# A fourth expert with 64 token slots, large and small experts in strict alternation, and a general path per expert

## The chip, the cores and the metric

The kernel runs on one core of a Trainium2 chip. The metric is device time in microseconds (us) of one execution. Three executions of the kernel before took 1542.57, 1547.81 and 1548.6 us (median 1547.81). The execution whose trace is read here took 1543.95 us; its span, from the first to the last instruction, is 1542.2 us, so 1.75 us lie around the span.

## The reference

Two decoder layers over 256 positions of width 1024, in float32. Layer 0 has dilated attention and a dense mixer, layer 1 has windowed attention with sinks and a mixer of eight experts, of which each token takes two:

```python
def _moe(h, w_router, w1, w3, w2):
    logits = (h @ w_router).astype(jnp.float32)
    top_v, top_i = lax.top_k(logits, TOP_K)           # 2 of 8
    wts = jax.nn.softmax(top_v, axis=-1)
    gates = jnp.einsum('bske,bsk->bse', one_hot(top_i, N_EXPERTS), wts)
    y = jnp.zeros_like(h)
    for e in range(N_EXPERTS):
        y = y + gates[..., e:e + 1] * _swiglu(h, w1[e], w3[e], w2[e])   # (silu(h w1) * (h w3)) w2
    return y
```

Each expert has w1 and w3 of 1024 x 3584 and w2 of 3584 x 1024, 42 MiB in all. The 256 tokens make 512 choices, 64 per expert on average. On the inputs of the reference the experts 0 to 7 get 65, 75, 60, 89, 63, 65, 47 and 48 tokens. After the experts comes a gated projection of a per-layer embedding and a last RMSNorm.

## The kernel before, in words

Both layers run on one core, stage after stage. The change touches the last stage, the experts, which begins about 617 us into the span and ends about 1492 us.

**Slots and ranks.** `route` counts the tokens of each expert and ranks the experts by that count; expert 0 always stands at rank 0, and the others follow from the fullest down. `CAPS` gives each rank its slots, 96 or 64: five ranks have 96 and three 64. `TURNS` is the order in which ranks take their turn: 0, 5, 1, 2, 6, 3, 4, 7. With L for 96 slots and S for 64 that is L S L L S L L S.

**A turn.** `Expert.gather` picks an expert's tokens with one-hot matmuls (tile P, result xb). `hidden` multiplies them by w1 and w3 (result H), `hidden_tail` applies silu and the product and transposes (tiles sa, sb, hT), `output` multiplies by w2 (result Y), `combine` scatters Y back to the tokens (tiles yh, yl, PT) and adds it to x. The 3584 columns are done in four chunks, three of 1024 and one of 512; `hidden` of a chunk runs ahead of `output` of the chunk before. The tokens are the stationary operand, in groups of 32: a matmul of `mm32` holds 32 tokens and streams a weight tile's columns past them, and four of them run side by side on the array. A turn with 96 slots has three groups and three banks of H, one with 64 has two groups and two banks.

**Weights.** Each weight goes over the array straight from its load buffer (`next_raw`). A tile is 1 MiB, 42 per turn. The buffers are `raw` (5), `mwa` (2) and `mwb` (10). SyncE (SP in the trace) issues all loads in one order, each into the buffer that comes free next. In the last turn the pool `mwb` ends (`moe_cut`), so that the last 14 tiles of the experts and the four of the gate projection go through 7 buffers. Which expert a rank is, SyncE reads from the tensor `cnt` (`find`).

**The general path.** If any expert has more tokens than its slots (`most > 0`), `beyond(1)` goes over all eight experts again for the tokens left over, and `beyond(2)` once more if over 96 are left. Every engine loads `most` and branches. An engine that skips the branch waits on its own semaphores and adds to them what the branch would have added; SyncE waits there for all of its loads issued so far.

**Order.** `Flow` lays out the instructions by planned times while the program is built: TensorE's order (H, Y, gathers, combines) is fixed then, and each wait is a semaphore. SyncE's loads have no planned time; they follow as buffers come free.

Of the kernel before, what the change touches and what calls it, by code (L numbers as in the profile page):

```python
# [13 lines left out]
I32 = mybir.dt.int32  # L14
AF = mybir.ActivationFunctionType
OP = mybir.AluOpType
# [4 lines left out]
S = 256  # L21
# [7 lines left out]
MOE_CHUNKS = ((0, 1024), (1024, 1024), (2048, 1024), (3072, 512))  # L29
NE = 8  # L30

CAPS = (96, 96, 96, 96, 96, 64, 64, 64)
TURNS = (0, 5, 1, 2, 6, 3, 4, 7)
CAP = 96
BIG = 512.0
NRAW = 5
# [308 lines left out]
def trunk(ctx, tc, x, p, attn_norm, ffn_norm, a_w_qkv, a_w_o, kv_norm, kv_w, b_w_q, b_sinks,  # L345
          b_w_o, dense_w1, dense_w3, dense_w2, moe_router, moe_w1, moe_w3, moe_w2,
          ple_norm, ple_w_gate, ple_w_proj, final_norm, masks, rope, mats, lessm, out):
    nc = tc.nc
    ctx.enter_context(tc.manual_schedule())
    flow = Flow()  # L350
    scal = Timed(flow, "act", nc.scalar, act_cost)
    act = scal.activation
    vec = Timed(flow, "vec", nc.vector, vec_cost)
# [10 lines left out]
    def pool(name, bufs, stack=ctx, **kw):  # L364
        return stack.enter_context(tc.tile_pool(name=name, bufs=bufs, reuse_waits="tile", **kw))
# [7 lines left out]
    rt = pool("rt", 1)  # L373
# [4 lines left out]
    st = Stream(nc, scal, vec, flow, rawp, 3, 2048)  # L378
# [39 lines left out]
    def add_moe(s, seq, at=None, extra=None):  # L418


        prev = None
        where = 0

        for j, item in enumerate(list(seq) + [None]):
            if item is not None:
                e, f0, fn = item
                r0 = f0 * D // fn
                for r in range(0, D, s.width * 128 // fn):
                    for w in (moe_w1, moe_w3):
                        s.add((expert_tile(w, e, (r0 + r) * fn // 128, s.width), s.width // fn), "raw")  # L430
            if j == at:
                s.add(extra, "raw")
                where = len(s.specs)
            if prev is not None:
                e, f0, fn = prev
                for r in range(f0, f0 + fn, s.width * 128 // D):
                    s.add((expert_tile(moe_w2, e, r * D // 128, s.width), s.width // D), "raw")
            prev = item
        return where

    def moe_seq(es):
        return [(e, f0, fn) for e in es for f0, fn in MOE_CHUNKS]
# [486 lines left out]
    if True:  # L929
# [122 lines left out]
        posm = rt.tile([128, NB, NE], F32, name="posm")  # L1052
        gates = rt.tile([128, NB, NE], F32, name="gates")
        rstat = rt.tile([128, 8], F32, name="rstat")
        cnt = rt.tile([128, 16], I32, name="cnt")
        by_rank = [rt.tile([128, NB, NE], F32, name=n) for n in ("posr", "gater")]
        count, total, capx, capt = (rt.tile([128, NE], F32, name=n) for n in ("count", "total", "capx", "capt"))
        for r, c in enumerate(CAPS):
            vec.memset(capt[:, r:r + 1], float(c))
# [254 lines left out]
    def experts(es, nxt=None, then={}, ahead=True):  # L1314

        E = {}
        nf = len(MOE_CHUNKS)

        def begin(i):
            E[i] = es[i]()  # L1320
            return E[i].gather()

        def products(i, res, f, Y):
            if i == len(es) - 1 and f == nf - 1:

                flow.until(lambda: res)
                st.hold = False
            output(E[i], Y, res, MOE_CHUNKS[f][1], f == 0, f == nf - 1)
            if f == nf - 1:
                flow.start(E[i].combine(Y, nxt if i == len(es) - 1 else None))  # L1330

        prev = None
        for i in range(len(es)):
            if i not in E:
                g = begin(i)
                if not E[i].ready:
                    flow.spawn(g)
            Y = [psY.tile([128, 512], F32, name=f"Y{k}", tag=f"Y{k}") for k in (range(3) if E[i].ng == 3 else (0,))]
            for f, (f0, fn) in enumerate(MOE_CHUNKS):
                res = []  # L1340
                g = begin(i + 1) if ahead and f == nf - 2 and i + 1 < len(es) else None
                hidden(E[i], fn, res)
                if (i, f) in then:
                    then[i, f]()
                if not ahead:
                    products(i, res, f, Y)
                    continue
                if g is not None:
                    flow.spawn(g)
                if prev is not None:  # L1350
                    products(*prev)
                prev = (i, res, f, Y)
            if not ahead:
                flow.drain()
        if ahead:
            products(*prev)
        flow.drain()

    def route():

        while 0 not in n_f1.chosen:
            yield flow.now + 100.0
        yield flow.due(sel)
        ps = acc()
        mm(ps[:, 0:8], tri, sel[:, 0], start=True, stop=False, skip_group_check=True)
        mm(ps[:, 8:16], ones, sel[:, 0], start=False, stop=False, skip_group_check=True)
        mm(ps[:, 16:24], ones, sel[:, 0], start=False, stop=False, skip_group_check=True)
        while 1 not in n_f1.chosen:
            yield flow.now + 100.0
        yield flow.due(sel)  # L1370
        mm(ps[:, 8:16], tri, sel[:, 1], start=False, stop=False, skip_group_check=True)
        mm(ps[:, 16:24], ones, sel[:, 1], start=False, stop=True, skip_group_check=True)
        vec.scalar_tensor_tensor(posm.rearrange(g16), sel.rearrange(g16), -BIG, ps[:, 0:16], op0=OP.mult, op1=OP.add)
        if WARM2:
            warm(WARM2)
        first.append(Expert(CAPS[0], posm[:, :, 0:1], by_rank[1][:, :, 0:1]))
        vec.tensor_copy(count, ps[:, 16:24])
        flow.start(first[0].gather())

        d8, a8, perm = d4[:, 0], a4[:, 0], d4[:, 1]  # L1380
        vec.tensor_copy(total, count)
        vec.memset(total[:, 0:1], 2.0 * S)
        vec.tensor_tensor(d8, total[:, None, :].to_broadcast([128, NE, NE]),
                          total[:, :, None].to_broadcast([128, NE, NE]), op=OP.subtract)
        d, a = d8.rearrange(f64), a8.rearrange(f64)
        vec.scalar_tensor_tensor(a, d, 0.0, less, op0=OP.is_equal, op1=OP.mult)
        vec.scalar_tensor_tensor(a, d, 0.0, a, op0=OP.is_gt, op1=OP.add)
        vec.tensor_reduce(rstat[:, 0:8], a8, axis=AX.X, op=OP.add)
        vec.tensor_scalar(rstat[:, 0:8], rstat[:, 0:8], -BIG, None, op0=OP.add)

        vec.tensor_tensor(perm, iota[:, 0:8][:, :, None].to_broadcast([128, NE, NE]),
                          rstat[:, None, 0:8].to_broadcast([128, NE, NE]), op=OP.is_equal)
        vec.tensor_tensor(a8, perm, iota[:, None, 0:8].to_broadcast([128, NE, NE]), op=OP.mult)
        vec.tensor_reduce(rstat[:, 0:8], a8, axis=AX.X, op=OP.add)
        vec.tensor_scalar(cnt[:, 0:8], rstat[:, 0:8], BIG, None, op0=OP.add)
        for tb in range(NB):
            vec.tensor_tensor(a8, perm, posm[:, tb, None, :].to_broadcast([128, NE, NE]), op=OP.mult)
            vec.tensor_reduce(by_rank[0][:, tb], a8, axis=AX.X, op=OP.add)

        vec.tensor_tensor(a8, perm.rearrange("p r e -> p e r"), capt[:, None, :].to_broadcast([128, NE, NE]), op=OP.mult)  # L1400
        vec.tensor_reduce(capx, a8, axis=AX.X, op=OP.add)
        vec.tensor_tensor(total, count, capx, op=OP.subtract)
        vec.tensor_reduce(rstat[:, 0:1], total, axis=AX.X, op=OP.max)
        vec.tensor_scalar(cnt[:, 8:9], rstat[:, 0:1], 0.0, None, op0=OP.max)

    def find_gates():

# [31 lines left out]
    def find():  # L1439

        for r in TURNS:
            if r:
# [8 lines left out]
    banks.close()  # L1451


    most = nc.values_load(cnt[0:1, 8:9], min_val=0, max_val=S,
                          skip_runtime_bounds_check_because="a count of at most 256 tokens")
    main = st

    def beyond(i):

        nonlocal st, selp  # L1460
        sel1 = selp
        with ExitStack() as es:
            selp = pool(f"sel_{i}", 1, es, side="right")
            expert_pools(es, es, f"_{i}")
            st = Stream(nc, scal, vec, flow, pool(f"raw_{i}", 2, es, side="right"), 0, 1024, 2)
            for item in moe_seq(range(NE)):
                add_moe(st, [item])
            for tb in range(NB):
                vec.tensor_tensor(posm[:, tb], posm[:, tb], capx, op=OP.subtract)
            if i == 1:  # L1470
                vec.memset(capx, float(CAP))
            experts([lambda e=e: Expert(CAP, *(v[:, :, e:e + 1] for v in (posm, gates))) for e in range(NE)], ahead=False)
        st = main
        selp = sel1

# [154 lines left out]
```

## Time and profile before

| | |
|---|---|
| three executions, us | 1542.57, 1547.81, 1548.6 |
| profiled execution, us | 1543.95 |
| its span, us | 1542.2 |
| mean granted TensorE clock | 0.99 |
| TensorE (PE) busy | 1500.6 us, 97% |
| VectorE (DVE) busy | 541.3 us, 35% |
| ScalarE (ACT) busy | 435.2 us, 28% |
| moved by DMA | 455.66 MB, mean 295 GB/s |

PE is the matmul itself and PEld the loading of its stationary operand. Matmul ends are modelled, so the pace of a group is read from its starts. Each matmul of `mm32` in the program stands twice in the trace. "SPq" is SyncE's queue of DMA issues. A wait is put down to the event that came last.

### The profile page before, as it was taken

To read this page: it belongs to the slowest core of one execution; us is meant where nothing else is said; L and a number is where in the kernel's file an instruction comes from. 1 tells how busy PE (TensorE), PEld (TensorE's weight loads), DVE (VectorE), ACT (ScalarE), POOL (GpSimd) and SP (SyncE) were. 2 spreads that over 40 slices of the span, in tenths; PEclk is the share of its full clock that TensorE was granted. 3 is DMA by queue.
4 is the path that set the end of the run, shared out by engine and by line. 5 is a ranking of instruction groups with operands and counts; after the bars stand their busy time and mean duration, and the time that the engine had idled before them with its cause. 6 is when DMAs were issued, how large, how long until landed. Compare 5 with 4: busy or idle time off the path is not lost.

```text
span 1542.2 us, 28405 instructions
## 1 busy us (share of the span) xinstructions
PE 1500.6 (97%) x11944; PEld 859.4 (56%) x11944; DVE 541.3 (35%) x1274; ACT 435.2 (28%) x852; POOL 11.3 (1%) x22
## 2 busy tenths in 40 slices
PE   7999999999999999799999999999999999999977
PEld 7999988888888887334324333334343343343335
DVE  6777777755454796210020100210201001201124
ACT  5555555564443766110000100110100010001124
POOL 0000000000000000000000000000000000000000
PEclk9999999999999999899999999999999999999988
DMA  9554444475455331999999999999999999999780
GB/s 280 157 144 139 129 123 148 134 276 186 170 186 197 134 113 55 364 385 421 421 421 419 421 420 421 420 395 362 422 420 420 421 420 420 401 356 408 320 341 28
DMA packets 163383, 455.66 MB, mean 295 GB/s; under 512 B 15440, under 2 KB 97232, under 8 KB 120240
## 3 DMA queue, kind: packets, MB, share of 16 engines
q1 hardware_dynamic: 162928, 453.31, 76.6%
q8 instruction: 95, 1.56, 0.4%
q0 software_dynamic: 176, 0.40, 0.1%
q14 instruction: 40, 0.33, 0.1%
q10 hardware_dynamic: 144, 0.07, 0.0%
HBM read 452.69 MB, written 1.05 MB: 294 GB/s over the span
## 4 chain that ended last, share of the span: by engine, by line
PE 56%; DVE 1%; DMA 1%; ACT 1%; issue 0%; POOLq 0%; DVEq 0%; ACTq 0%
PE H L1149 33%; PE Y L1149 16%; PE scr L356 4%; PE scr L1270 1%; PE acc L356 1%; DMA raw<-in_ple_w_gate 1%; DVE wlo L136 0%; PE scr L361 0%; ACT xb L136 0%; DVE x L136 0%; DVE gate L136 0%; DVE h L136 0%; ACT whi L136 0%; ACT gate L136 0%; DVE xT0l L136 0%
## 5 line engine op out<-in xcount | busy, mean ns | idle before, releaser
L1149 PE MATMUL H<-mwb,xb 128*32 128x512 f32 (+1 forms) x3208 | 328.0, 539 | 0.0
L136 DVE TENSOR_TENSOR wlo<-raw,whi 128x768 fp32r<-128x768 f32 (+1 forms) x180 | 188.6, 1080 | 117.7 <-ACT whi L136 117.0
L136 DVE TENSOR_TENSOR sa<-sa,H 128x512 f32<-128x512 f32 (+1 forms) x32 | 19.9, 622 | 586.3 <-PE H L1149 586.3
L1149 PEld LDWEIGHTS H<-mwb,xb 128*32 128x32 f32 x3208 | 106.6, 110 | 196.1 <-issue 174.2
L136 ACT ACTIVATE whi<-raw 128x768 fp32r<-128x768 f32 (+1 forms) x180 | 162.0, 945 | 110.8 <-PE scr L356 61.3
L136 ACT ACTIVATE sa<-H 128x512 f32<-128x512 f32 (+1 forms) x32 | 17.4, 544 | 612.8 <-PE H L1149 612.8
L1149 PE MATMUL H<-raw,xb 128*32 128x512 f32 (+1 forms) x1480 | 160.9, 549 | 7.8 <-DVE gates L136 7.8
L1149 PE MATMUL Y<-mwb,hT 128*32 128x512 f32 x1192 | 138.2, 594 | 0.0
L1149 PEld LDWEIGHTS H<-raw,xb 128*32 128x32 f32 x1480 | 50.2, 111 | 99.4 <-issue 82.7
L356 PE MATMUL acc<-whi,xT0h 128*128 128x384 f32 (+2 forms) x296 | 104.3, 352 | 0.0
L356 PE MATMUL acc<-wlo,xT0h 128*128 128x384 f32 (+2 forms) x296 | 102.0, 344 | 0.7 <-DVE wlo L136 0.7
L356 PE MATMUL acc<-whi,xT0l 128*128 128x384 f32 (+2 forms) x296 | 101.6, 343 | 0.1
L1149 PE MATMUL Y<-raw,hT 128*32 128x512 f32 x856 | 99.5, 594 | 0.5 <-DMA raw<-in_moe_w 0.5
L356 PE MATMUL acc<-whi,xT1h 128*128 128x384 f32 (+2 forms) x280 | 98.4, 351 | 0.3 <-ACT xT1h L136 0.3
L356 PE MATMUL acc<-whi,xT1l 128*128 128x384 f32 (+2 forms) x280 | 93.7, 335 | 0.2 <-DVE xT1l L136 0.2
L356 PE MATMUL acc<-wlo,xT1h 128*128 128x384 f32 (+2 forms) x280 | 93.5, 334 | 0.0
L1149 PEld LDWEIGHTS Y<-mwb,hT 128*32 128x32 f32 x1192 | 37.7, 110 | 79.9 <-issue 76.0
L1149 PE MATMUL H<-mwa,xb 128*32 128x512 f32 (+1 forms) x688 | 79.1, 528 | 0.0
L1149 PEld LDWEIGHTS Y<-raw,hT 128*32 128x32 f32 x856 | 27.3, 110 | 58.8 <-issue 55.8
L356 PEld LDWEIGHTS acc<-whi,xT0h 128*128 128x128 f32 x296 | 56.6, 191 | 4.6 <-issue 2.3
L356 PEld LDWEIGHTS acc<-wlo,xT0h 128*128 128x128 f32 x296 | 56.6, 191 | 3.6 <-DVE wlo L136 1.4
L356 PEld LDWEIGHTS acc<-whi,xT0l 128*128 128x128 f32 x296 | 56.5, 191 | 3.0 <-DVE xT0l L136 0.3
(220 smaller groups left out, 1865.2 us busy)
## 6 DMA issues: line engine op xcount, KB each, us to landing
mwb<-in_moe_w SPq DMA_DIRECT2D x190, 1024.0 KB, 16.1
raw<-in_moe_w SPq DMA_DIRECT2D x104, 1024.0 KB, 15.1
mwa<-in_moe_w SPq DMA_DIRECT2D x42, 1024.0 KB, 14.7
raw<-in_a_w_qkv SPq DMA_DIRECT2D x144, 256.0 KB, 4.0
raw<-in_dense_w SPq DMA_DIRECT2D x33, 1024.0 KB, 5.0
raw<-in_ple_w_gate SPq DMA_DIRECT2D x8, 1024.0 KB, 8.6
raw<-in_a_w_o SPq DMA_DIRECT2D x4, 1024.0 KB, 5.2
raw<-in_b_w_q SPq DMA_DIRECT2D x4, 1024.0 KB, 5.3
```

The lines of the kernel that those rows point to most:

```text
L136: f(*a, **k)
L356: nc.tensor.matmul(dst, lhsT, rhs, **kw)
L1149: nc.tensor.matmul(dst, xs, w, start=start, stop=stop)
L1270: nc.tensor.transpose(t[:, m * i:m * (i + 1)], v[:m, 128 * i:128 * (i + 1)], ident[:m, :m])
```

## The change

`CAPS` gets a fourth rank with 64 slots in place of 96 (rank 4), and `TURNS` becomes 0, 4, 1, 5, 2, 6, 3, 7, which is L S L S L S L S. In `route` a VectorE instruction writes each expert's overflow into `cnt`, which grows from 16 to 24 columns, ahead of the largest overflow. `beyond` reads an expert's own overflow on every engine and works on it inside an inner branch; it no longer goes over all eight in one stream.

```diff
-CAPS = (96, 96, 96, 96, 96, 64, 64, 64)
-TURNS = (0, 5, 1, 2, 6, 3, 4, 7)
+CAPS = (96, 96, 96, 96, 64, 64, 64, 64)
+TURNS = (0, 4, 1, 5, 2, 6, 3, 7)
...
-        cnt = rt.tile([128, 16], I32, name="cnt")
+        cnt = rt.tile([128, 24], I32, name="cnt")
...
         vec.tensor_tensor(total, count, capx, op=OP.subtract)
+        vec.tensor_scalar(cnt[:, 8:16], total, 0.0, None, op0=OP.max)
         vec.tensor_reduce(rstat[:, 0:1], total, axis=AX.X, op=OP.max)
-        vec.tensor_scalar(cnt[:, 8:9], rstat[:, 0:1], 0.0, None, op0=OP.max)
+        vec.tensor_scalar(cnt[:, 16:17], rstat[:, 0:1], 0.0, None, op0=OP.max)
...
-    most = nc.values_load(cnt[0:1, 8:9], min_val=0, max_val=S,
+    most = nc.values_load(cnt[0:1, 16:17], min_val=0, max_val=S,
...
-            st = Stream(nc, scal, vec, flow, pool(f"raw_{i}", 2, es, side="right"), 0, 1024, 2)
-            for item in moe_seq(range(NE)):
-                add_moe(st, [item])
+            rawq = pool(f"raw_{i}", 2, es, side="right")
...
-            experts([lambda e=e: Expert(CAP, *(v[:, :, e:e + 1] for v in (posm, gates))) for e in range(NE)], ahead=False)
+            for e in range(NE):
+                left = nc.values_load(cnt[0:1, 8 + e:9 + e], min_val=0, max_val=S,
+                                      skip_runtime_bounds_check_because="a count of at most 256 tokens")
+                with tc.If(left > CAP * (i - 1)):
+                    st = Stream(nc, scal, vec, flow, rawq, 0, 1024, 2)
+                    for item in moe_seq([e]):
+                        add_moe(st, [item])
+                    experts([lambda: Expert(CAP, *(v[:, :, e:e + 1] for v in (posm, gates)))], ahead=False)
```

On TensorE, the end of the second chunk of the fourth turn stood as follows in the kernel before (H with three banks of which the last two are seen, Y with three, and the transposes of sa and sb):

```order
L1149 MATMUL H_22383<-mwb,xb 32x512 x4
L1149 MATMUL H_22384<-mwb,xb 32x512 x4
L1149 MATMUL Y_21609<-mwb,hT 32x512 x4
L1149 MATMUL Y_21611<-mwb,hT 32x512 x4
L1149 MATMUL Y_21610<-mwb,hT 32x512 x4
L1270 MATMUL scr<-ident,sa 128x128 x4
L1270 MATMUL scr<-ident,sb 128x64 x4
L1149 MATMUL Y_21609<-mwb,hT 32x512 x4
```

In the changed kernel the same place, where the Y rows still belong to the third turn, reads:

```order
L1149 MATMUL H_22511<-mwb,xb 32x512 x4
L1149 MATMUL H_22512<-mwb,xb 32x512 x4
L1149 MATMUL Y_21738<-mwb,hT 32x512 x4
L1149 MATMUL Y_21740<-mwb,hT 32x512 x2
L1270 MATMUL scr<-ident,sa 128x128 x4
L1149 MATMUL Y_21740<-mwb,hT 32x512 x2
L1149 MATMUL Y_21739<-mwb,hT 32x512 x4
L1149 MATMUL Y_21738<-mwb,hT 32x512 x4
```

The third bank of H and the transpose of sb are gone from the fourth turn. The other turns have the instructions that a turn of their size had before, in the new sequence.

On VectorE, at the end of `route`, ahead of the load of `most` and the branch (a piece of the difference; L1454 and L1455 are the load, L1476 and L1482 the branch):

```order
 L136 TENSOR_REDUCE capx<-a_5666 128x8
 L136 TENSOR_TENSOR total<-count,capx 128x8
+L136 TENSOR_SCALAR cnt<-total 128x8
 L136 TENSOR_REDUCE rstat<-total 128x1
 L136 TENSOR_SCALAR cnt<-rstat 128x1
 L136 CAST PT<-scr 96x256
-L1454 TENSOR_LOAD cnt
-L1476 COMPARE_AND_BRANCH
+L1455 TENSOR_LOAD cnt
+L1482 COMPARE_AND_BRANCH
```

One instruction is added ahead of the branch. Behind the branch SyncE's loads, up to the end of the kernel, stand in the same order and in the same buffers as before; only the experts that the registers name differ.

## Rows read from the trace of the kernel before

**Rows 1.** The page: busy time by engine; then GB/s in 40 slices.
```profile
PE 1500.6 (97%) x11944; PEld 859.4 (56%) x11944; DVE 541.3 (35%) x1274; ACT 435.2 (28%) x852; POOL 11.3 (1%) x22
...
GB/s 280 157 144 139 129 123 148 134 276 186 170 186 197 134 113 55 364 385 421 421 421 419 421 420 421 420 395 362 422 420 420 421 420 420 401 356 408 320 341 28
```

**Rows 2.** Windows of the expert stage: length, busy of each engine, clock, DMA share, GB/s.
```profile
650.00:660.00 10.00, 10.00 (x100) 3.15 (x96) 0.64 (x1) 1.88 (x2) 0.00 (x0) 1.00 0.37 126
660.00:1000.00 340.00, 339.40 (x3298) 120.43 (x3294) 39.16 (x71) 27.30 (x50) 0.00 (x0) 1.00 1.01 421
1000.00:1080.00 80.00, 79.89 (x820) 30.42 (x816) 7.25 (x16) 5.49 (x11) 0.00 (x0) 1.00 0.96 381
1080.00:1330.00 250.00, 249.52 (x2374) 86.58 (x2370) 34.02 (x56) 21.23 (x38) 0.00 (x0) 1.00 1.01 420
1330.00:1400.00 70.00, 69.89 (x734) 27.49 (x730) 5.36 (x14) 4.89 (x10) 0.00 (x0) 1.00 0.93 368
1400.00:1447.00 47.00, 47.00 (x408) 14.32 (x404) 9.71 (x14) 5.43 (x9) 0.00 (x0) 1.00 1.01 421
1447.00:1469.00 22.00, 22.00 (x160) 7.77 (x156) 0.69 (x1) 3.47 (x6) 0.00 (x0) 1.00 0.51 200
```

**Rows 3.** Waits of SyncE's queue, 617 to 1500 us: total, times, longest.
```profile
SPq L233 <- PE H L1149: 252.5, 111, 5.7
SPq L233 <- PE Y L1149: 162.2, 77, 6.9
```

**Rows 4.** TensorE's timeline: the gathers of four turns (start, length, tiles).
```profile
916.92 2.02 PE L356 MATMUL scr<-P,xn 128*128 128x96 f32 x16
1037.86 2.00 PE L356 MATMUL scr<-P,xn 128*128 128x64 f32 x16
1133.93 2.02 PE L356 MATMUL scr<-P,xn 128*128 128x96 f32 x16
1241.20 2.02 PE L356 MATMUL scr<-P,xn 128*128 128x96 f32 x16
```

**Rows 5.** The chain that ended last: one chunk of each size (start, length).
```profile
693.23 20.60 PE H L1149 x192
719.14 10.44 PE Y L1149 x96
...
1120.26 13.73 PE H L1149 x128
```

**Rows 6.** The end of the last turn on TensorE's timeline, then on SyncE's.
```profile
1489.91 1.92 PE L1149 MATMUL Y<-raw,hT 128*32 128x512 f32 x16 [0.47 <-DMA raw<-in_moe_w]
1496.55 0.79 PE L356 MATMUL scr<-yh,PT 64*128 64x512 f32 x1 [4.72 <-ACT yh L136]
...
1438.57 2.77 SPq L233 DMA_DIRECT2D mwa<-in_moe_w  x2
1465.93 7.80 SPq L233 DMA_DIRECT2D raw<-in_moe_w  x5
```

**Rows 7.** The chain that ended last, behind the experts.
```profile
1480.32 12.25 DMA raw<-in_ple_w_gate
```

**Rows 8.** VectorE ahead of the branch and TensorE behind it, on the timeline.
```profile
630.35 0.16 DVE L136 TENSOR_REDUCE rstat<-total 128x1 f32<-128x8 f32 x1
630.54 0.15 DVE L136 TENSOR_SCALAR cnt<-rstat 128x1 int32<-128x1 f32 x1
...
637.90 2.79 PE L1149 MATMUL H<-raw,xb 128*32 128x512 f32 x12 [7.83 <-DVE gates L136]
```

**Rows 9.** Windows of TensorE alone: length, busy, clock, DMA share, GB/s.
```profile
16.00:620.00 604.00, 598.08 (x3498) 1.00 0.51 159
...
637.00:641.00 4.00, 3.10 (x16) 0.53 1.02 418
641.00:660.00 19.00, 19.00 (x184) 1.00 0.68 261
1491.00:1511.00 20.00, 11.45 (x37) 0.58 0.46 170
```

**Rows 10.** TensorE's timeline in layer 1, a wait short of 1 us.
```profile
552.11 0.55 PE L361 MATMUL scr<-ident,qk 128*128 128x128 f32 x3 [0.80 <-DVE qk L136]
```

## The prediction

> **What bounds the kernel now.** I read the page first, then stretches, then who waits for whom. On the page TensorE looks like the bound (97% busy), but the row of GB/s stands at 420 or 421 through most of the expert stage [rows 1]. Two limits lie close together there, and the question is which ends last. The windows tell [rows 2]: TensorE is busy without a break from 660 us to 1469 us, while the transfers run at 420 to 421 GB/s with DMA share 1.01 and fall below in three places only: 381 GB/s in 1000 to 1080, 368 in 1330 to 1400, 200 in 1447 to 1469. A fourth, 126 GB/s in 650 to 660, has another cause (below). SyncE's longest waits are for TensorE's H and Y, 414.7 us together [rows 3]: it waits for buffers. TensorE waits for a load once, 0.47 us at the last tile of w2 [rows 6]. So TensorE sets the end of this stage, and the loads follow it, but they have little room: the three dips are all the time that they could still win.
>
> They are worth 80 x (1 - 381/421) = 7.6 us, 70 x (1 - 368/421) = 8.8 us and 22 x (1 - 200/421) = 11.5 us, 27.9 us in sum.
>
> **What TensorE saves.** The period of a turn is read from gather to gather [rows 4]; each stands in the turn before its own. From 916.92 to 1037.86 lies one large turn, 120.9 us. From 1037.86 to 1241.20 lie a large and a small one, 203.3 us, so a small turn is 82.4 us. The change makes one large turn small: 38.5 us less. The count agrees: a large chunk has 192 H matmuls in 20.60 us and 96 Y in 10.44 us, a small one 128 H in 13.73 us [rows 5]. Over 3.5 chunks' worth, H falls from 72.1 to 48.1 us and Y by a third of 36.5, 12.2 us; these 36.2 us and the transposes of sb that go make up the 38.5. Every junction that the new order has (large to small, small to large, small at the end) exists before, and TensorE passes each of them without a wait, so I add nothing for the sequence of instructions.
>
> **What the loads allow.** A tile is 1,048,576 bytes, at 420 GB/s 2.497 us, and a turn is 42 tiles, 104.9 us. In a large turn (120.9) the loads gain 16.0 us on TensorE, in a small one (82.4) they lose 22.5. Full buffers are 17 tiles, 42.5 us ahead; then SyncE waits and the rate dips. Before, each pair of large turns gains 32.0 us; the dip of 7.6 says that the loads stood 24.4 us under full after the first small turn, so 1.9 under full after the first large turn. From there the new order gives, in us under full after each turn: 1.9, 24.4, 8.4, 30.9, 14.9, 37.4, 21.4, 43.9. It never comes to full, so the two middle dips go. With 2 tiles held by the running matmuls, TensorE runs dry at about 37.5 under full: for moments at the end of the sixth turn, for 43.9 - 37.5 = 6.4 us in the last.
>
> The third dip comes from the 7 buffers of the last stretch: SyncE had issued its load at about 1441 and waited until 1465.93 [rows 6], since the loads were far ahead when `mwb` ended. With the new order they enter the last turn 21.4 us under full, 42.5 - 21.4 = 21.1 us or 8 tiles ahead, and have lost about half of 22.5 more by its middle: some 10 us, 4 tiles, under the 7 buffers. So this dip goes too.
>
> **The sum.** Two ways lead to the end of the last Y. By TensorE: it ended its last Y at 1491.83 (1489.91 + 1.92) [rows 6]; less 38.5, plus 6.4 to 8 of new waiting, 1459.7 to 1461.3. By the loads: the last tile came at 1489.91, less 27.9 is 1462.0; plus 1.9 for its matmuls, 1463.9. The later one holds: 1463.9, which is 27.9 us earlier. The gain is cut from 38.5 by the loads.
>
> Behind the last Y lie 1542.2 - 1491.8 = 50.4 us. There the chain runs through the gate projection's first load, issued 1480.32, taking 12.25 us [rows 7], right behind the last w2 tile. It follows that tile by the same queue in both kernels, so I keep the 50.4 us.
>
> The span is then 1514.3 us, the profiled execution 1543.95 - 27.9 = 1516.0. The added VectorE instruction stands ahead of the branch, where its neighbours take 0.16 us and start 0.19 us apart [rows 8]: 0.2 us, on TensorE's path to the first H, though the loads don't wait for it. Bounds: 0, if the loads alone end last, and 0.5 with its semaphore. The inner branches and their loads of a register lie inside the outer branch, which isn't taken: on these inputs the ranks from 1 on have 89, 75, 65, 63, 60, 48, 47 tokens for 96, 96, 96, 64, 64, 64, 64 slots, and expert 0 has 65 for 96. The skipped side does what it did before plus one wait and one addition per engine on a semaphore of its own; bounds 0 and 0.5 us, and I take 0, since SyncE there waits for its loads anyway, which is the dip at 650 to 660, kept as it is. Behind a skipped branch TensorE starts 7.83 us late [rows 8]; the jump is over a block of similar size, so no change, bounds 1 us each way.
>
> With 1 us for the interplay at the end, the profiled execution comes to 1517. The median of three executions lay 3.9 us above the profiled one, so the same gain from there is 1519.9. I predict 1518.
>
> **A rule on the ceiling of the loads.** The rows show 420 to 421 GB/s in every stretch that isn't held up, large or small turns alike, at share 1.01 [rows 2]. The Trainium skill, page "DMA: Bandwidth & Descriptors", section "Specifications", gives a fabric ceiling of 435 GB/s and a limit of HBM per core of about 358. The trace passes the second by 62 GB/s, so I don't use it. By the first a tile could take an estimated 2.41 us, 29 us less over 336 tiles, and the whole of TensorE's saving would come through: rival 1.
>
> **Rivals.**
>
> 1. The loads aren't at their limit, and TensorE's 38.5 us come through whole: 1518 - 10.6 = 1507. For it: TensorE never waits before. Against it: SyncE has several loads outstanding all the time and the rate doesn't pass 421.
>
> 2. The pause at the 7 buffers stays, since the loads are further ahead than I count: 11.5 us of the gain are lost, 1529.5. It decides if more than 7 tiles are ahead at the middle of the last turn, against 4 by my count. Errors of 1 us per turn would add up to 3 tiles, so it isn't far.
>
> 3. Slower: TensorE's clock. It stands at 1.00 from 16 to 620 us, and falls to 0.53 and 0.58 behind waits of 7.83 and 4.72 us [rows 6, 8, 9], that is about 1.2 of 2.4 GHz. In the changed kernel TensorE waits for loads for the first time, in small pieces through the last turns. If that held it at the lower level for the whole last small turn, the 48.1 us of H and 24.3 of Y would double: 72.4 us more, less the 22.5 by which the loads exceed that turn, 50 us: 1568. It decides once more than 30 us net are lost so. Against it: a wait of 0.80 us at 552 didn't lower the clock [rows 9, 10], and after 637.9 the clock was back within 4 us. The Trainium skill, page "TensorE: Matmul & The Clock Gate", section "HAM oscillation — how this bites in real kernels", tells of a kernel whose clock fell again at each wait for a load, tile after tile; it is this rival's mechanism, and no wait in the trace of before has this pattern.
>
> 4. No change: the rate falls when TensorE reads at its heels. At 397 GB/s (2.64 us) 190 tiles from 1000 us on would take 27 us more, the whole gain: 1544. Against it: the same 420 beside large and small turns.
>
> 5. The change doesn't do what it says: a fifth-ranked expert with over 64 tokens would send its 42 MiB once more through two buffers, at least 105 us: about 1625. The count is 63, so two choices would have to fall differently.
>
> **How the numbers follow.** Forecast 0.73; rival 1 0.06; rival 2 0.11; rival 3 0.05; rival 4 0.04; rival 5 0.01. The forecast's own range is 1512 to 1525: 3 us of spread between executions to each side, and 2 to 3 us for the waits in the last turns. The range of 1507 to 1531 takes in rivals 1 and 2. A measurement of this kernel tells about 0.5%, 8 us, from no change. Forecast and rivals 1 and 2 are faster by more than that, 0.90, of which I take 0.01 for noise beside rival 2; rival 4 is the core of "same", 0.05; rivals 3 and 5 are slower, 0.06.
>
> **What would show it.** Right: the gathers' periods stay 120.9 and 82.4 us in the first five turns, 203 us per pair; the rate stays at 420 from 660 us to the last tile, with no dip near 1040, 1370 or 1455; TensorE shows waits for loads of about 1 to 3 us, 5 to 10 us in sum, nearly all in the last three turns; the last Y ends near 1464 and the rest takes 50 us. Wrong: a dip of the rate before the last tiles (rival 2), a granted clock under 1.00 between 1200 and 1460 (rival 3), a rate above 425 or no wait for loads at all (rival 1), loads of 128 x 1024 behind the branch (rival 5). If TensorE waits and the loads dip in the same stretch, my account of the lead is wrong.

## The result: 1523.4 us, 1.4% faster, and the profile after

| | before | after |
|---|---|---|
| median, same rounds, us | 1547.69 | 1523.36 (1521.61 to 1523.9, 4 runs) |
| ratio (95% interval) | | 0.9857 (0.9842 to 0.9872) |
| profiled execution, us | 1543.95 | 1523.48 |
| its span, us | 1542.2 | 1521.6 |

Forecast: 1518, range 1507 to 1531. A second set of five runs on another occasion gave 1522.84 (ratio 0.9845, 0.9832 to 0.9859). The profiled execution gained 20.5 us, the medians 24.3, since the profiled execution of before was 3.7 us under its median.

The page of after, TensorE's busy time and GB/s in 40 slices (beside [rows 1]):

```profile
PE 1465.9 (96%) x11562; PEld 846.1 (56%) x11562; DVE 533.4 (35%) x1263; ACT 431.3 (28%) x846; POOL 11.3 (1%) x22
...
GB/s 276 161 138 140 142 128 146 109 284 182 182 191 166 147 158 56 298 321 420 421 420 421 420 421 420 421 420 420 420 420 420 420 420 421 420 420 420 386 354 28
```

The slices with 395, 362, 401, 356 and 408 are gone; one with 386 is left near the end. The windows of after, cut as in [rows 2] (length, busy of PE, PEld, DVE, ACT, POOL, clock, DMA share, GB/s):

```profile
650.00:660.00 10.00, 10.00 (x100) 2.83 (x96) 0.00 (x0) 1.28 (x1) 0.00 (x0) 1.00 0.33 134
660.00:1000.00 340.00, 339.62 (x3292) 120.11 (x3288) 41.42 (x75) 28.26 (x52) 0.00 (x0) 1.00 1.01 418
1000.00:1080.00 80.00, 78.85 (x774) 29.75 (x770) 6.96 (x11) 5.85 (x11) 0.00 (x0) 1.00 1.01 420
1080.00:1330.00 250.00, 242.84 (x2320) 84.61 (x2316) 26.96 (x50) 17.95 (x33) 0.00 (x0) 1.00 1.01 420
1330.00:1400.00 70.00, 69.88 (x724) 27.15 (x720) 8.59 (x15) 6.70 (x13) 0.00 (x0) 1.00 1.01 420
1400.00:1447.00 47.00, 44.87 (x346) 14.36 (x342) 5.19 (x8) 5.89 (x10) 0.00 (x0) 1.00 0.96 392
1447.00:1469.00 22.00, 19.30 (x239) 7.12 (x230) 0.42 (x1) 0.77 (x2) 0.00 (x0) 1.00 1.00 411
```

The two dips in the middle have gone entirely. Where 200 GB/s stood at the end there is a small one, 392 and 411. TensorE is no longer busy without a break: 242.84 of 250 us in 1080 to 1330. Its waits for loads in 617 to 1480 us (total, times, longest), and below them SyncE's in the same stretch (beside [rows 3]):

```profile
PE H L1149 <- DMA mwb<-in_moe_w: 7.8, 7, 1.5
PE H L1149 <- DMA raw<-in_moe_w: 2.5, 2, 1.3
PE Y L1149 <- DMA mwa<-in_moe_w: 1.2, 2, 0.6
PE Y L1149 <- DMA mwb<-in_moe_w: 0.9, 2, 0.6
PE Y L1149 <- DMA raw<-in_moe_w: 0.8, 2, 0.5
```

```profile
SPq L233 <- DMA mwb<-in_moe_w: 287.1, 150, 3.4
SPq L233 <- DMA raw<-in_moe_w: 146.7, 77, 3.5
SPq L233 <- PE H L1149: 78.5, 56, 4.8
SPq L233 <- PE Y L1149: 49.2, 30, 6.9
```

The roles are exchanged. TensorE waits 13.2 us for loads, SyncE's waits for H and Y fall from 414.7 to 127.7 us, and SyncE now waits chiefly for earlier loads to land. The gathers (beside [rows 4]):

```profile
919.96 2.00 PE L356 MATMUL scr<-P,xn 128*128 128x64 f32 x16
1015.91 2.03 PE L356 MATMUL scr<-P,xn 128*128 128x96 f32 x16
1124.43 2.00 PE L356 MATMUL scr<-P,xn 128*128 128x64 f32 x16
1223.69 2.02 PE L356 MATMUL scr<-P,xn 128*128 128x96 f32 x16
1336.24 2.00 PE L356 MATMUL scr<-P,xn 128*128 128x64 f32 x16
```

Here every period runs from a large turn to a small one or back (96.0, 108.5, 99.3 and 112.6 us), so the periods of 120.9 and 82.4 us that the prediction named as a sign don't appear, and only a pair compares with its 203.3 us: 204.5 from 919.96 to 1124.43 and 211.8 from 1124.43 to 1336.24. Most of the growth is the waits for loads in those stretches (1.0 and 6.9 us). TensorE's timeline in the last turn (in brackets the idle time before), and SyncE's (beside [rows 6]):

```profile
1427.73 3.64 PE L1149 MATMUL H<-mwb,xb 128*32 128x512 f32 x32 [0.78 <-DMA mwb<-in_moe_w]
1432.72 2.78 PE L1149 MATMUL H<-mwb,xb 128*32 128x512 f32 x24 [1.35 <-DMA mwb<-in_moe_w]
1435.43 7.13 PE L356 MATMUL scr<-raw,pT 128*128 128x512 f32 x16
...
1470.02 1.92 PE L1149 MATMUL Y<-raw,hT 128*32 128x512 f32 x16 [0.48 <-DMA raw<-in_moe_w]
```

```profile
1427.81 2.83 SPq L233 DMA_DIRECT2D mwa<-in_moe_w  x2
1442.60 7.80 SPq L233 DMA_DIRECT2D raw<-in_moe_w  x5
```

The last Y ends at 1471.94. TensorE waits for loads at 1427 and 1432, and at the same time SyncE pauses from 1430.6 to 1442.60: the `raw` buffer that it wants next is held by the projection of the per-layer embedding, 7.13 us at 1435.43. SyncE's waits in 1425 to 1470 us say the same, 4.5 us for the projection's own tile to land and 7.3 us for its matmuls:

```profile
SPq L233 <- PE scr L356: 7.3, 1, 7.3
...
SPq L233 <- DMA raw<-in_ple_w_proj: 4.5, 1, 4.5
```

### The profile page after: what moved, and what is told of

It reads as the page before. It is cut to its first block, busy times and chain, and to the rows that moved or that the text cites. A ratio compares the mean times of both kernels' runs of the same rounds, so it can differ in the third digit from the quotient of the medians.

```text
span 1521.6 us, 27622 instructions
## 1 busy us (share of the span) xinstructions
PE 1465.9 (96%) x11562; PEld 846.1 (56%) x11562; DVE 533.4 (35%) x1263; ACT 431.3 (28%) x846; POOL 11.3 (1%) x22
## 4 chain that ended last, share of the span: by engine, by line
PE 39%; DMA 17%; DVE 1%; ACT 0%; issue 0%; POOLq 0%; SPq 0%; DVEq 0%; ACTq 0%
PE H L1149 23%; DMA mwb<-in_moe_w 13%; PE Y L1149 10%; PE scr L356 3%; DMA raw<-in_moe_w 2%; DMA mwa<-in_moe_w 1%; PE acc L356 1%; PE scr L1270 1%; DMA raw<-in_ple_w_gate 1%; DVE wlo L136 0%; PE scr L361 0%; DVE x L136 0%; DVE gate L136 0%; ACT xb L136 0%; DVE h L136 0%
## 5 line engine op out<-in xcount | busy, mean ns | idle before, releaser
L1149 PE MATMUL H<-mwb,xb 128*32 128x512 f32 (+1 forms) x3056 | 313.6, 539 | 7.8 <-DMA mwb<-in_moe_w 7.8
L136 DVE TENSOR_TENSOR sa<-sa,H 128x512 f32<-128x512 f32 (+1 forms) x32 | 19.9, 621 | 582.7 <-PE H L1149 582.7
L1149 PEld LDWEIGHTS H<-mwb,xb 128*32 128x32 f32 x3056 | 101.6, 110 | 195.6 <-issue 163.1
L1149 PE MATMUL Y<-mwb,hT 128*32 128x512 f32 x1136 | 131.6, 594 | 0.9 <-DMA mwb<-in_moe_w 0.9
L1149 PE MATMUL H<-mwa,xb 128*32 128x512 f32 (+1 forms) x608 | 73.0, 537 | 0.0
```

Of the source, the lines that this page charges most:

```text
L136: f(*a, **k)
L1149: nc.tensor.matmul(dst, xs, w, start=start, stop=stop)
```

## Experiments

**Which part does it: the general path alone, the slots and turns alone.** First the new `beyond`, overflow columns and registers with the old tables:

```diff
-CAPS = (96, 96, 96, 96, 64, 64, 64, 64)
-TURNS = (0, 4, 1, 5, 2, 6, 3, 7)
+CAPS = (96, 96, 96, 96, 96, 64, 64, 64)
+TURNS = (0, 5, 1, 2, 6, 3, 4, 7)
```

> The general path of the changed kernel and its added VectorE instruction, with the slots and turns of the kernel before. Theory A: nothing of it lies on the path when no expert overflows, so 1547.7 within 3 us, with TensorE's last Y near 1492 to 1495. Rival C (the new general path alone moved the expert stage's start by the 2.9 us that the trace of the changed kernel shows): the first H 2 to 3 us later than in the kernel before in every execution, time about 1550.5.

Measured: 1545.93 us against 1544.81, ratio 1.0007 (0.9997 to 1.0016). Then the new tables with the old `route` and `beyond`:

> The slots and turns of the changed kernel with the general path of the kernel before. Theory A: all of the gain, 1523.4 within 1.5 us. Rival C (the new general path starts the expert stage 2 to 3 us late): 1520.5, with the loads after the branch beginning near 657 us and not 660.6.

Measured: 1522.24, ratio 0.9848 (0.9831 to 0.9866). The slots and turns make the gain. The untaken general path costs nothing that these times can show: alone, where TensorE still ends last, under 2.5 us by its interval, and beside the new slots 1523.36 stands against 1522.24, with overlapping intervals of the ratios. The traces do show something. SyncE's first loads behind the skipped branch in the kernel before, with the slots alone (old path) and with the general path alone:

```profile
657.18 2.04 SPq L233 DMA_DIRECT2D raw<-in_moe_w  x4
```

```profile
657.57 2.00 SPq L233 DMA_DIRECT2D raw<-in_moe_w  x4
```

```profile
659.39 1.94 SPq L233 DMA_DIRECT2D raw<-in_moe_w  x4
```

The loads restart between 657.03 and 657.57 us in all three traces with the old path skipped, and between 658.27 and 660.58 in all seven with the new one as the change has it. In the general path alone TensorE ends last, which hides this. Why the restart is later isn't shown.

**Same slots, another order.** L S L L S L S S instead of strict alternation:

```diff
-TURNS = (0, 4, 1, 5, 2, 6, 3, 7)
+TURNS = (0, 4, 1, 2, 5, 3, 6, 7)
```

> Four small turns as in the changed kernel, but with two large turns in a row twice: L S L L S L S S in place of L S L S L S L S. Theory A (the loads end last; what counts is that they are never held up): the pair of large turns fills the 17 buffers again, the loads dip near 1050 us by some 5 to 8 us, and the last two small turns leave TensorE waiting longer (15 to 20 us in sum against 13). Time 1523.4 + 5 to 8, 1528 to 1531. Rival B (TensorE ends last, and the turns' order is nothing): the same work on TensorE, 1523.4 within 1 us.

Measured: 1526.3 (1525.45 to 1527.86), ratio 0.9878 (0.9861 to 0.9895), 4.1 us above the slots alone in the same rounds. The windows of this kernel where the second pair of large turns stands, and at the end:

```profile
1000.00:1080.00 80.00, 79.89 (x818) 30.60 (x818) 7.38 (x16) 5.48 (x11) 0.00 (x0) 1.00 0.98 391
...
1400.00:1447.00 47.00, 38.14 (x272) 11.39 (x268) 1.37 (x2) 4.87 (x9) 0.00 (x0) 0.96 1.00 413
```

The dip after two large turns is back (391 GB/s, 80 x (1 - 391/421) = 5.7 us), and TensorE waits near the end instead (38.14 of 47 us busy). Here the time that the loads stand still while the buffers are full isn't made up later. My account had the direction and the place right; the size is smaller than I expected.

**Less work for TensorE.** Three more experts at 64 slots. It leaves out the tokens beyond 64 of ranks 1 to 3 and sets the overflow to 0, so that no general path follows:

```diff
-CAPS = (96, 96, 96, 96, 64, 64, 64, 64)
+CAPS = (96, 64, 64, 64, 64, 64, 64, 64)
...
-        vec.tensor_scalar(cnt[:, 16:17], rstat[:, 0:1], 0.0, None, op0=OP.max)
+        vec.tensor_scalar(cnt[:, 16:17], rstat[:, 0:1], 0.0, 0.0, op0=OP.max, op1=OP.mult)
```

> Seven small turns behind the first large one; the tokens beyond 64 of an expert are left out and the largest overflow is set to 0, so that the general path is not taken. TensorE's work falls by another 3 x 38.5 = 115 us against the changed kernel. Theory A (the loads already end last there): 1520 to 1524, with TensorE waiting about 125 us for loads in sum and the rate at 420 GB/s from 661 us on, but for the pause of some 3 us near 1435. Rival B (TensorE still ends last, its waits being a small matter): some 40 us or more faster, under 1485. Rival D (many waits lower TensorE's clock): windows with a granted clock under 1.00 between 800 and 1460 us.

Measured: 1521.31 (1521.01 to 1521.7), ratio 0.9844 (0.9828 to 0.9861). TensorE is busy 90 us less by the page (1375.7), and the time is the same to 1 or 2 us. The largest of its waits for loads in 660 to 1470 us:

```profile
PE H L1149 <- DMA mwb<-in_moe_w: 54.8, 45, 2.5
PE H L1149 <- DMA raw<-in_moe_w: 23.8, 20, 1.4
PE H L1149 <- DMA mwa<-in_moe_w: 9.8, 8, 1.9
```

The matmuls that go are replaced by waits for loads (101 us over all tiles, 98 of them; 125 us were expected). In the changed kernel the loads bind.

**More loads, in the changed kernel and in the one before.** One more tile of 1 MiB in each turn, loaded and never read, 8 in all:

```diff
                 e, f0, fn = item
                 r0 = f0 * D // fn
+                if f0 == MOE_CHUNKS[1][0]:
+                    s.add((expert_tile(moe_w2, e, 0, s.width), s.width // D), "raw")
...
+                if f == 1:
+                    st.next_raw()
                 hidden(E[i], fn, res)
```

> The changed kernel with one more 1 MiB load in each of the eight turns, into the ordinary buffers, that no matmul reads. Theory A (the loads end last): each costs its 2.5 us whole, 20.0 us in sum, 1523.4 + 20 = 1543, within 2 us; TensorE's waits for loads grow from 13 to some 30 us. Rival B (TensorE ends last): under 5 us more.

> The kernel before with the same eight loads more, 20.0 us of transfers. Theory A (there TensorE ends last and the loads have 27.9 us of pauses to spare): the pauses near 1040, 1370 and 1455 shrink by about 17 us in sum and the time stays, 1544.8 + 0 to 3 us. Rival E (both limits already bind there, so that the gain of the change is only its fewer large turns): about 20 us more, 1565.

Measured in the changed kernel: 1543.65, ratio 0.9992 (0.9982 to 1.0001). Against the changed kernel's own 1523.36, which is of other rounds, that is 20.3 us (20.9 by the two ratios), 8 x 2.5, the full price. In the kernel before: 1551.99, ratio 1.0047 (1.003 to 1.0064), 6.8 us, more than the 0 to 3 that I expected and a third of the full price. Its windows over the three dips:

```profile
1000.00:1080.00 80.00, 79.89 (x818) 30.64 (x818) 7.38 (x16) 5.48 (x11) 0.00 (x0) 1.00 1.00 409
...
1330.00:1400.00 70.00, 69.89 (x728) 27.44 (x724) 6.63 (x15) 5.48 (x11) 0.00 (x0) 1.00 0.99 400
...
1447.00:1469.00 22.00, 22.00 (x187) 7.00 (x186) 0.69 (x1) 1.94 (x4) 0.00 (x0) 1.00 0.69 276
```

By the sums of [rows 2] the dips are now 2.3, 3.5 and 7.6 us, 13.4 in place of 27.9: 14.5 of the added 20 us went into them. TensorE waits for no load from 617 to 1490 us in this trace, so the loads aren't what made it slower. In its profiled execution the span grew by 8.4 us; TensorE began the stage 1.9 us later and waits 4.1 us at combines and transposes. That the planned order moved them when a buffer was taken in it is likely, but not shown. The other 2 us I can't place.

**The pause at the projection.** Keep the pool `mwb` in use until the w1 and w3 tiles of the last chunk are issued, one step after the projection:

```diff
+        st.hold = True
+
+    def end_mwb():
+        nonlocal xtpool
         st.ahead_raw(st.used)
         mws.close()
...
-    by_turn(TURNS, {(NE - 1, PLE_AT - 1): load_p1, (NE - 1, PLE_AT): proj_p1}, nxt=n_p1.half)
+    by_turn(TURNS, {(NE - 1, PLE_AT - 1): load_p1, (NE - 1, PLE_AT): proj_p1, (NE - 1, PLE_AT + 1): end_mwb}, nxt=n_p1.half)
```

> The changed kernel with the pool of ten buffers kept one chunk longer in the last turn, to the tiles of w1 and w3 of its last chunk: eight tiles more go through 17 buffers in place of 7. Theory A with the pause near 1435 put down to the 7 buffers, of which one is held through the 7.1 us of the projection's matmuls: the dip in 1430 to 1450 us (3.3 us) goes, and the time falls by about 3 us, to 1519 to 1521. Rival F (the pause costs nothing, since something behind it ends last): 1523.4 within 1 us.

Measured: 1522.73, ratio 0.9857 (0.984 to 0.9873): no gain. SyncE's timeline in it:

```profile
1427.69 2.93 SPq L233 DMA_DIRECT2D mwa<-in_moe_w  x2
1432.79 2.88 SPq L233 DMA_DIRECT2D mwb<-in_moe_w  x2
1442.59 7.80 SPq L233 DMA_DIRECT2D raw<-in_moe_w  x5
```

Two more loads went out at 1432.79, and still the next waits for the projection's `raw` buffer until 1442.59, since SyncE issues in one order. The tiles behind it stood no earlier: the last Y begins at 1470.02 in both. That only the count of buffers made this pause is refuted; that it is the buffer held by the projection fits the waits shown above, but a kernel in which it lets go earlier wasn't run. A lack of buffers can make a pause too: in the kernel before with added loads the projection's tile lies in `mwb`, and SyncE waits up to 18.7 us for an H instead.

**Registers ahead of the branch.** The seven loads with which SyncE reads the experts' ranks from `cnt`, put ahead of the skipped branch instead of behind it. This kernel was run twice, the second time beside the changed kernel itself:

```diff
+    find()
     most = nc.values_load(cnt[0:1, 16:17], min_val=0, max_val=S,
...
     find_gates()
-    find()
```

> The changed kernel with SyncE's seven register loads of the experts' numbers put ahead of the branch, where SyncE would wait for its loads anyway. Behind the branch they stand between the last landing and the next load, 658.34 to 660.46 us. Theory A (the loads' restart is on the path): 2.2 us faster, about 1521, with the first load behind the branch 2.2 us nearer to the landing that frees it. Rival F (the restart is hidden by what lies loaded): 1523.4 within 1 us.

> h_early once more, beside the changed kernel on the same chip. Theory A: 2.2 us faster than after_again, 1521 against 1523, first load behind the branch within 0.1 us of the last wait there (660.58 - 658.29 = 2.3 us in the changed kernel). Rival F: no difference beyond 1 us.

> The changed kernel once more, for comparison with the kernel of h_early on the same chip. Its gain over the kernel before in the same rounds: theory A 22 to 25 us. The stage before the experts decides when TensorE starts: the first H between 637 and 641 us, as the piece of lowered clock near 620 us is 0, 3.4 or 6.8 us long in the traces so far.

Measured: 1521.36 at first (ratio 0.9853, 0.9837 to 0.987); then 1521.26 (1520.04 to 1521.98) against 1522.84 (1522.31 to 1523.62) for the changed kernel, ratios 0.9836 (0.9823 to 0.985) and 0.9845 (0.9832 to 0.9859). SyncE's first loads behind the branch in the second set, the changed kernel's row first:

```profile
660.21 3.26 SPq L233 DMA_DIRECT2D raw<-in_moe_w  x4
```

```profile
656.49 1.99 SPq L233 DMA_DIRECT2D raw<-in_moe_w  x4
```

3.7 us earlier, and the span ends 3.2 us earlier (1518.3 against 1521.5), while TensorE's first H of the stage stands at nearly the same time (637.73 against 637.57); the medians differ by 1.6 us. The five runs of each don't overlap, but the intervals of the ratios do, so the size is open. In the profiled execution of the repeated changed kernel TensorE began the stage 3.2 us earlier than in the first one (637.57 against 640.76), while the loads restarted at 660.21 against 660.58, and the spans are equal (1521.5, 1521.6): the span follows the loads, not TensorE's start. Seven traces agree: the changed kernel twice, the slots alone, the three more small experts, the pool kept longer and the early registers twice. From the first load into `mwb` behind the branch to the end of the span they take 857.0 to 858.0 us, wherever the first H stands between 637.57 and 640.99. A late TensorE acts through the buffers: with the slots alone the loads restarted early, at 657.57, but waited for H until 663.26, and the span is 1521.1.

**What the general path costs when it is taken.** Only three ranks with 96 slots, so that rank 3 has 65 tokens for 64, with the old path and then with the new:

```diff
-CAPS = (96, 96, 96, 96, 64, 64, 64, 64)
-TURNS = (0, 4, 1, 5, 2, 6, 3, 7)
+CAPS = (96, 96, 96, 64, 64, 64, 64, 64)
+TURNS = (0, 3, 1, 4, 2, 5, 6, 7)
```

> Slots 96, 96, 96 and five times 64 with turns L S L S L S S S, with the general path of the kernel before: rank 3 has 65 tokens, one over its slots, so that the branch is taken and all eight experts are gone over again. Each loads 84 half tiles through two buffers, at least 105 us at 420 GB/s, and TensorE's 109 us of a large turn hardly overlap: 105 to 300 us per expert, 840 to 2400 us over 1523, 2360 to 3920.

> The same slots and turns with the general path of the changed kernel: only the one expert that overflows is gone over again. Theory: an eighth of the excess of i_over_old, 105 to 300 us, plus under 10 us for seven inner branches not taken; 1630 to 1830. Rival: each inner branch costs as much as the outer one (7 to 8 us of TensorE's time, and SyncE waits for its loads), so 60 us more than an eighth.

Measured: 4365.21 and 1910.64. Against the changed kernel's 1523.36 that is 2842 and 387 us more, the first 355 per expert; these slots and turns without an overflow weren't run. Both are above what I expected. A stretch of TensorE's timeline in the new path:

```profile
800.07 5.35 PE L1149 MATMUL H<-raw,xb 128*32 128x512 f32 x24 [4.07 <-DMA raw<-in_moe_w]
809.62 4.36 PE L1149 MATMUL H<-raw,xb 128*32 128x512 f32 x24 [4.20 <-DMA raw<-in_moe_w]
817.52 5.35 PE L1149 MATMUL H<-raw,xb 128*32 128x512 f32 x24 [3.55 <-DMA raw<-in_moe_w]
```

With two buffers of 512 KB, work and waiting take turns: about 5 us of matmuls, then some 4 us idle. The matmuls are slow as well, 24 of H in 5.35 us, where the changed kernel took 2.78 at 1432.72: TensorE is at the lower clock, 0.50 in a window from 800.07 to 805.40, 0.80 on average over these 50 us:

```profile
800.00:850.00 50.00, 29.82 (x172) 6.93 (x174) 1.80 (x3) 1.78 (x3) 0.00 (x0) 0.80 0.40 134
```

From the path's gather at 664.03 to its end at 1015.76 lie 351.7 us, of which TensorE waits 134.2 for loads. The other 217, some 11 us of other waits among them, are twice the 109 us that I had put for the work of a large turn. With 109 it would have come to some 250 us, inside my 105 to 300 (an estimate from these rows). Its loads on the page (size, us from issue to landing):

```profile
raw<-in_moe_w SPq DMA_DIRECT2D x84, 512.0 KB, 4.1
```

The wait is about the time that a load takes to land. 84 loads at 355/84 = 4.2 us on average make an expert. TensorE is back at the main experts at 1029.66, 388.9 us later than in the changed kernel. One overflowing expert costs 355 us and some 32 for the branches around it, between the under 10 that I expected and the 60 of the rival; the old path paid for eight.

## Why the prediction was right, point by point

- **What binds.** Right: before, TensorE has the last word and the loads have 28 us of slack, of which the added loads took 14.5 without a wait of TensorE for a load; after, the loads bind. The added loads show both sides (20.3 us after, 6.8 before), and taking 90 us from TensorE moves the time by only 1 to 2 us.
- **TensorE's 38.5 us.** From its first H of the stage to the end of the last Y TensorE takes 853.9 us before and 831.2 after. Less 0.5 and 13.2 us of waits for loads, that is 853.4 and 818.0: 35.4 us saved. The sum by chunks (36.2) was nearer than the one by gathers; where the other 3 us went isn't shown. It didn't matter, since the loads end last.
- **The three dips, 27.9 us.** This is the term that was mis-sized most. From the restart behind the branch (657.18 before, 660.58 after) to the last tile (1489.91, 1470.02) the loads take 832.7 and 809.4 us: 23.3 won. The two middle dips went as forecast. Of the third, 47 x (1 - 392/421) + 22 x (1 - 411/421) = 3.8 us are left by these windows, a rival 2 in small. About 1 us stays open. The prediction put this dip down to the number of buffers and the loads' lead, and missed what held the next buffer. In the kernel before it was the projection as well: the longest of SyncE's waits for it, 22.7 us, ended when its matmuls did, at 1465.9 (SyncE's waits in 617 to 1500):

```profile
SPq L233 <- PE scr L356: 23.0, 2, 22.7
```

A smaller lead makes the pause shorter, 12.0 us in place of 24.6, and doesn't end it.
- **The lead.** Under-full amounts of 37.4 and 43.9 us after the sixth and the last turn: TensorE waits 6.9 us around the end of the sixth (1214 to 1258) and 5.3 in the last, and already 1.0 at 1044, at the end of the fourth. In sum 13.2 instead of 6.4 to 8. The later restart explains little of it: the loads restarted 3.4 us later than in the trace of before, but TensorE began 2.9 us later too, which leaves 0.5. What was mis-sized is the point at which TensorE runs dry. The waits of 1.0, 6.9 and 5.3 us against 30.9, 37.4 and 43.9 under full put it at about 30 us, not at 37.5 (an estimate from these waits): some 5 tiles of the 17 were of no use to TensorE, where I had counted 2. The sign by which my account would be wrong was seen, at 1430 to 1442: TensorE had been waiting, yet a buffer was held. The account counts full buffers and leaves out who holds one.
- **The start of the stage** I had kept. In the profiled executions the first H came 2.9 us later and the loads restarted 3.4 us later; the second is the difference between 23.3 and the 19.9 us by which the last Y came earlier. The first H isn't the change: with the general path alone it comes at 637.71, in the repeated changed kernel at 637.57, with the slots alone at 640.87. The loads' restart goes with the general path: with its registers behind the branch, 0.7 to 3.6 us later in every trace that skips the new one than in those that skip the old one; with the registers ahead of the branch it came at 655.88 and 656.49. This is the second term that was mis-sized: the prediction took 0 for the skipped path, with 0.5 as its bound, since SyncE waits there anyway.
- **The tail**, 50.4 us kept: 49.7, with the same first load of the gate projection at its head, 11.20 us in place of 12.25 [rows 7]:

```profile
1462.33 11.20 DMA raw<-in_ple_w_gate
```

- **The sum.** 23.3 - 3.4 + 0.7 = 20.6 us of span against 27.9, so the profiled execution came 6.5 us above the 1517 that I gave it, and the median 5.4 above 1518. The mechanism held; the size fell short, by the third dip and the restart.
- **Rivals.** 1 is out: the rate stays at 420 to 421, and more room on TensorE doesn't raise it. The Trainium skill, page "DMA: Bandwidth & Descriptors", section "Specifications", has a ceiling of 435; no window of 40 us or more of ours passes 421, and windows of 4 us show up to 426. 2 holds for 3 to 4 of its 11.5 us. 3 is out for the changed kernel: the clock is 1.00 in every window from 650 to 1469, with waits up to 1.5 us. Where the waits are 4 us long, in the general path, its mechanism is there. 4 is out: 420 GB/s while TensorE reads at the loads' heels. 5 didn't happen, and its price was far too low: I gave at least 105 us and a time of about 1625, the run shows 387 more, 1911.

## What to carry to other kernels

Where two limits lie within a few per cent of each other, price a saving on the one by the slack of the other: here the sum of the dips in the load rate (28 us) and not TensorE's 38.5. From that slack take what other users of the buffers hold: with loads issued in one order, a single buffer that another user still needs stops all of them (24.6 us before, 12.0 after). Which limit binds is told best by two cheap kernels, one that adds a known amount of load and one that takes away work: in a kernel bound by its loads the first moves the time by its full price, the second hardly at all. And test a part that should cost nothing where its cost would show: the general path alone was run in a kernel bound by TensorE, which hides a later restart of the loads.

## What I had not expected of the hardware

- In the changed kernel 15 waits of up to 1.5 us left TensorE's clock at 1.00. Waits of that length don't always do so: of the two executions of the kernel with early registers, each with a wait of 1.53 us ahead of 1252, one shows 1.00 and the other 0.57 in 1252 to 1256, and the other order of turns shows 0.69 in 1436 to 1440. With three more small experts (98 waits of up to 2.5 us) windows at five places show the lower level, two of them (length, busy, clock, DMA share, GB/s):

```profile
963.00:967.00 4.00, 4.00 (x19) 0.57 1.02 420
1069.00:1073.00 4.00, 4.00 (x18) 0.57 1.02 426
```

  It cost nothing there, the loads being the bound; in a kernel bound by TensorE it would.
- When the stage begins varies by 3.8 us between executions (first H 637.22 with the other order, 640.99 with the pool kept longer), along with a stretch near 620 to 627 us in which TensorE is at the lower clock for longer, for less long or not at all. In the changed kernel's two profiles, the windows of the same 4 us, the later start first:

```profile
620.00:624.00 4.00, 3.66 (x11) 0.50 1.00 418
```

```profile
620.00:624.00 4.00, 3.25 (x15) 1.00 1.02 426
```

  What sets its length stays open.
- A path with two load buffers moves 120 to 134 GB/s over stretches of 300 to 400 us, under a third of what 17 buffers reach: its matmuls and loads take turns, and the waits of about 4 us between them go with a granted clock of 0.74 to 0.78 over these stretches.
